# Weight blocks split into two parts in one step, and their products ordered by part

## The chip, the cores and the metric

The kernel runs on one core of a Trainium2 chip. The metric is the device time of one execution in microseconds; the time before is the median of three runs.

## The reference

One layer on 256 tokens of width 2048, all in float32: a normalisation, a projection `w_in` whose columns feed a gated delta net (8 heads of 128) and an RWKV7 part (16 heads of 64), an output projection `w_out`, a cross attention to 256 memory tokens (4 heads of 128), a feed-forward with squared ReLU, and a last normalisation:

```python
u = rmsnorm(h, mix_norm_w);  p = u @ w_in
o_dn = deltanet_group(p[..., :DN_COLS], ...)
o_rw = rwkv7_group(p[..., DN_COLS:], ...)
h = h + concatenate([o_dn, o_rw]) @ w_out
h = h + memory_cross_attention(rmsnorm(h), rmsnorm(mem), wq, wk, wv, wo)
h = h + square(relu(rmsnorm(h) @ ffn_w1)) @ ffn_w2       # 2048 -> 8192 -> 2048
return rmsnorm(h, final_norm_w)
```

## The kernel before

Every large product is made of float32r products. An operand x is split into a high part (x cast to float32r) and a low part (x less that, cast again); the sum of high x high, high x low and low x high stands for the float32 product. The activations are split once per use; the weights are split block by block as they come.

A block of weights is 512 KB, 128 partitions of 1024 values. `weights` loads it on SyncE's queue into one of five `raw` buffers (pool `wp`) and splits it in two steps of 512 values: a ScalarE copy (line 239) makes the high part `whi`, a VectorE subtraction (line 240, recorded at line 110 of the helper `tt`) the low part `wlo`. Each has three buffers (`WB`) of half a block. Loads and splits have a raised priority in the planner, the Tile framework's list scheduler, which sets the order on every engine from a simulated timeline.

`gemm` (line 244) computes 256 tokens by 512 columns into two PSUM banks, one for each 128 tokens. A block holds two k tiles of 512 columns. For each k tile and each half of the tokens it issues three products with the activations as the stationary operand and 512 weight columns moving: high x `whi` (line 254), high x `wlo` (255), low x `whi` (256): twelve a block. `gemm` serves `w_in` (112 blocks), `w_out` (32), `wk`, `wq`, `wv`, `wo` (8 each) and the second feed-forward layer `w2` (120; its last 8 blocks go through `gemm_rows`, which the change leaves alone).

`gemm_T` (line 261) computes the first feed-forward layer transposed, 128 hidden columns a bank. Here the weights are stationary and the activations move; a block holds eight k tiles of 128 columns. For each k tile it issues the low part against the high activations, 256 wide (line 272), and the high part against both parts of the activations, 512 wide (line 273); only at the first k tile of a bank does the low one come second (line 275). Two blocks make a bank, four banks a call, 16 calls: 128 blocks.

The feed-forward goes in four rounds of four `gemm_T` calls (32 blocks) and four `gemm` calls (32 blocks). Before it stand the scans of the two mixing groups, whose small products the planner places between those of `w_in`, `wk` and `w_out`. For `wk` and `wv` the memory's transpose is loaded in four tiles each (line 995) through the same `raw` buffers, as are two tiles of the scans' outputs (line 980); at the start three of the five buffers hold weights of the low-rank projection (line 352). ScalarE and VectorE also scale, shift and take results from PSUM.

Of the kernel before, what the change touches and what calls it, by code (L numbers as in the profile page):

```python
# [17 lines left out]
P = 128  # L18
# [9 lines left out]
WB = 3  # L28
# [12 lines left out]
def host_layout(inp):  # L41
    a = {k: np.asarray(v) for k, v in inp.items()}
    x, mem = a["x"][0], a["mem"][0]
    f = np.float32

    def tr(t):
        return np.ascontiguousarray(t.T.reshape(NKT, P, S).transpose(1, 0, 2))

    def blocks(w, n=NB):
        k, cols = w.shape  # L50
        return np.ascontiguousarray(
            w.reshape(k // (KB * P), KB, P, cols // n, n).transpose(3, 0, 2, 1, 4))

    def blocks_T(w):
        """[512 columns, 128 columns, half of the k tiles, p, k tile, column]"""
        return np.ascontiguousarray(w.reshape(2, 8, P, w.shape[1] // NB, 4, P).transpose(3, 4, 0, 2, 1, 5))

    w_in = a["w_in"][0]
    DN, RW = 0, 4112
    order = []  # L60
    for g in range(2):
        for j in (0, 1):
            u = 2 * g + j
            order += list(range(RW + 256 * u, RW + 256 * (u + 1)))
            order += list(range(RW + 1024 + 256 * u, RW + 1024 + 256 * (u + 1)))
            if j == 0:
                order += list(range(RW + 2048 + 512 * g, RW + 2048 + 512 * (g + 1)))
    for g in range(2):
        for j in range(3):
            order += list(range(1024 * j + 512 * g, 1024 * j + 512 * (g + 1)))  # L70
    order += list(range(3072, 4096))
    lora = list(range(RW + 3072, RW + 3328)) + list(range(4096, 4112))

    def col(v):
        return v.reshape(-1, P).T

    mu = a["rw_mu"][0]
    cols = np.concatenate([
        col(a["mix_norm_w"][0]), col(a["xa_norm_w"][0]), col(a["mem_norm_w"][0]), col(a["ffn_norm_w"][0]),
        a["dn_conv_w"][0].reshape(4, 24, P).transpose(2, 1, 0).reshape(P, 96),  # L80
        col(mu[0:1024]), col(mu[1024:2048]), col(mu[2048:3072]), col(mu[3072:3328]),
        col(a["rw_w0"][0]), col(a["rw_a0"][0]), col(a["rw_k_k"][0]), col(a["rw_k_a"][0]),
        col(a["rw_ln_w"][0]), col(a["rw_ln_b"][0]), col(a["rw_r_k"][0].reshape(-1)), col(a["dn_norm_w"][0]),
    ], axis=1)
    i = np.arange(P)
    bones = (i[:, None] // 64 == i[None, :] // 64).astype(f)
    consts = np.concatenate([
        np.eye(P, dtype=f), (i[:, None] <= i[None, :]).astype(f), bones, np.ones((P, P), f),
        np.tile(np.eye(16, dtype=f).reshape(1, 256), (P, 1)),
        (i[:, None] // 64 == np.arange(2)[None, :]).astype(f),  # L90
        (i[:, None] // 16 % 2 == np.arange(2)[None, :]).astype(f)], axis=1)
    r = {
        "xT": tr(x), "memT": tr(mem), "x": x, "mem": mem,
        "w_lora": blocks(w_in[:, lora], LORA), "w_in": blocks(w_in[:, order]),
        "w_out": blocks(a["w_out"][0]), "wq": blocks(a["xa_wq"][0]), "wk": blocks(a["xa_wk"][0]),
        "wv": blocks(a["xa_wv"][0]), "wo": blocks(a["xa_wo"][0]),
        "w1": blocks_T(a["ffn_w1"][0]), "w2": blocks(a["ffn_w2"][0]),
        "cols": cols, "wa2": np.concatenate([a["rw_w2"][0], a["rw_a2"][0]]),
        "g2": a["rw_g2"][0], "dnrow": np.concatenate([a["dn_a_log"][0], a["dn_dt_bias"][0]])[None, :],
        "fnw": a["final_norm_w"][None, :], "consts": consts,  # L100
    }
    return {k: np.ascontiguousarray(v) for k, v in r.items()}


def body(ctx, tc, I, out, dbg=None, upto=99):
# [24 lines left out]
    wp = ctx.enter_context(tc.tile_pool(name="wp", bufs=5))  # L130
# [14 lines left out]
    def bank(tag=None):  # L145
        """a PSUM bank: three serve the large products, two each of two scans, one the projections."""
# [24 lines left out]
    # derived per-channel scalars  # L171
# [15 lines left out]
    def lhs_split(raws, wname, pool, tag):  # L187
        """raw^T (times the norm's weight) split in two float32r parts, four k tiles a tile, as they are asked for."""
# [16 lines left out]
    def gemm_rows(lhs, wblk, evac, kbs, his, los):  # L205
        """the same, the first 128 tokens before the others, from weights that all stay."""
# [21 lines left out]
    def weights(src, a, b, parts):  # L228
        """a block of weights [128, a, b] in two float32r parts."""
        with tc.high_priority(3000):  # L230
            raw = wp.tile([P, a, b], F32, tag="raw", name=nm("raw"))
            nc.sync.dma_start(out=raw, in_=src)
            res = []
            n = a // parts
            for q in range(parts):
                hi = wp.tile([P, n, b], F32R, tag="whi", bufs=WB, name=nm("whi"))
                lo = wp.tile([P, n, b], F32R, tag="wlo", bufs=WB, name=nm("wlo"))
                w = raw[:, q * n:(q + 1) * n]
                A.copy(hi, w)  # L239
                tt(lo, w, hi.bitcast(F32), ALU.subtract)  # L240
                res += [(hi[:, i], lo[:, i]) for i in range(n)]
        return res

    def gemm(lhs, wblk, n, evac, kbs=None):
        """[256 tok, n] = lhs^T @ W: three float32r products stand for the float32 one."""
        acc = [bank("g") for _ in range(2)]
        kbs = list(kbs if kbs is not None else range(NKT // KB))
        for kb in kbs:
            w = weights(wblk[kb], KB, n, KB)
            for q in range(KB):  # L250
                for m in range(2):
                    first, last = kb == kbs[0] and q == 0, kb == kbs[-1] and q == KB - 1
                    xh, xl = lhs(kb * KB + q, m)
                    T.matmul(acc[m][:, :n], lhsT=xh, rhs=w[q][0], start=first, stop=False)  # L254
                    T.matmul(acc[m][:, :n], lhsT=xh, rhs=w[q][1], start=False, stop=False)  # L255
                    T.matmul(acc[m][:, :n], lhsT=xl, rhs=w[q][0], start=False, stop=last)  # L256
                    if last:
                        evac(m, acc[m][:, :n])


    def gemm_T(rhs, wblk, evac):
        """(x W)^T in four parts of 128 columns, [128 col, (W x_hi, W_hi x_lo)]; rhs(kt) is (x_hi, x_lo)^T, 512 wide."""
        for j in range(4):
            acc = bank("g")
            for b in range(2):
                w = weights(wblk[j, b], 8, P, 2)
                for k in range(8):
                    first, last = b == 0 and k == 0, b == 1 and k == 7
                    x = rhs(8 * b + k)
                    xf = x.rearrange("p a t -> p (a t)")  # L270
                    if not first:
                        T.matmul(acc[:, 0:S], lhsT=w[k][1], rhs=x[:, 0], start=False, stop=False)  # L272
                    T.matmul(acc, lhsT=w[k][0], rhs=xf, start=first, stop=last)  # L273
                    if first:
                        T.matmul(acc[:, 0:S], lhsT=w[k][1], rhs=x[:, 0], start=False, stop=False)
# [23 lines left out]
    def rms(src, name):  # L299
        """1 / rms of the rows of src[:, m, :]."""  # L300
# [8 lines left out]
    def tpose4(o, ins):  # L309
        """up to four 128x128 transposes into one bank."""  # L310
# [50 lines left out]
    # the clock of the array rises and the functions' table loads while the first operands are on their way  # L361
# [73 lines left out]
    # gates of the deltanet: [tok, chunk, head]  # L435
# [35 lines left out]
    inv = [0]  # L471

    def inverse(B, pool, pool2):
        """B is overwritten with the inverse of I + (its strictly upper part); what lies below its diagonal is zero.

        X12 = -X11 B12 X22 for blocks of 2 to 128, the larger ones on tiles of the array."""
# [11 lines left out]
        def quarters(t, n):  # L488
            """the quarters 11, 12, 22 of the diagonal blocks of 2n: [q, block, row, column]."""
# [94 lines left out]
    def rw_shift(pt, c0, names, blks):  # L584
        """columns c0.. of the projection [tok, col] to shifted [col, tok] tiles of two blocks."""
# [12 lines left out]
    def rw_unit(u, r, k, v):  # L598
# [59 lines left out]
        # bonus * v  # L658
# [8 lines left out]
        # scores  # L667
# [21 lines left out]
        # [tok, .] forms  # L689
# [57 lines left out]
        # group norm, bonus, gate  # L747
# [94 lines left out]
    def dn_unit(g, kq, v2):  # L842
# [6 lines left out]
        # norms per token: [tok, (k/q), chunk, head]  # L849
# [21 lines left out]
        # decays, scores  # L871
# [72 lines left out]
        # norm over the head, times silu(z)  # L944
# [90 lines left out]
    def tok_T(src, wname):  # L1035
        """transposes of src [tok, 2048] (times the norm's weight), split in two parts, four k tiles a step."""
# [131 lines left out]
    def last(m, p):  # L1168
        """the last 512 columns in two halves, so that little is left to do once the second's sum of squares is there."""
# [55 lines left out]
```

## Time and profile before

| | |
|---|---|
| median of three runs | 1446.87 us (1446.61 to 1447.17) |
| profiled execution, from first to last instruction (span) | 1442.5 us |
| what the median has over this span | 4.4 us |
| TensorE, VectorE, ScalarE busy | 98%, 66%, 54% |
| TensorE weight loads busy | 81% |
| weight blocks that `weights` splits | 424 |
| instructions | 22496 |

The profile has no time of its own for the profiled execution beside its span, so the span is set against the median of the runs. A matmul's record lasts until its result is drained, so records overlap, and the pace of TensorE is read from start to start and not from their length.

### The profile page before, as it was taken

To read this page: it belongs to the slowest core of one execution; us is meant where nothing else is said; L and a number is where in the kernel's file an instruction comes from. 1 tells how busy PE (TensorE), PEld (TensorE's weight loads), DVE (VectorE), ACT (ScalarE), POOL (GpSimd) and SP (SyncE) were. 2 spreads that over 40 slices of the span, in tenths; PEclk is the share of its full clock that TensorE was granted. 3 is DMA by queue.
4 is the path that set the end of the run, shared out by engine and by line. 5 is a ranking of instruction groups with operands and counts; after the bars stand their busy time and mean duration, and the time that the engine had idled before them with its cause. 6 is when DMAs were issued, how large, how long until landed. Compare 5 with 4: busy or idle time off the path is not lost.

```text
span 1442.5 us, 22496 instructions
## 1 busy us (share of the span) xinstructions
PE 1414.8 (98%) x8284; PEld 1168.9 (81%) x8284; DVE 950.1 (66%) x1799; ACT 780.8 (54%) x1491; POOL 50.6 (4%) x66
## 2 busy tenths in 40 slices
PE   9999999999999989999999999999999999999997
PEld 7877788787876868887788888888888888888886
DVE  7748574869587685767676655666556665566664
ACT  7656454555456454566565544555445554455553
POOL 0010001100010000000000000000000000000000
PEclk9999999999999999999999999999999999999999
DMA  7444433454366464556465556555665555655554
GB/s 281 157 145 152 135 121 112 147 177 144 102 200 207 138 190 146 166 173 212 136 209 186 190 192 197 185 187 189 193 197 186 185 190 194 195 182 187 191 188 146
DMA packets 90688, 252.88 MB, mean 175 GB/s; under 512 B 20673, under 2 KB 29393, under 8 KB 90193
## 3 DMA queue, kind: packets, MB, share of 16 engines
q1 hardware_dynamic: 70304, 243.96, 51.2%
q10 hardware_dynamic: 19920, 6.42, 1.8%
q8 instruction: 65, 1.06, 0.3%
q0 software_dynamic: 352, 1.06, 0.2%
q14 instruction: 47, 0.38, 0.1%
HBM read 244.72 MB, written 6.69 MB: 174 GB/s over the span
## 4 chain that ended last, share of the span: by engine, by line
PE 82%; DMA 7%; DVE 6%; ACT 3%; issue 2%; SPq 0%; POOL 0%; ACTq 0%; POOLq 0%; DVEq 0%
PE ps_g L273 16%; PE ps_g L255 16%; PE ps_g L254 15%; PE ps_g L256 15%; PE ps_g L272 8%; DVE wlo L110 2%; PE ps_s L675 2%; DMA scr<-Sc 1%; DMA xc<-inv 1%; DMA mraw<-in_memT_dram 1%; PE ps_x L312 1%; DMA g<-scr 1%; DVE xtmp L110 1%; DMA junk<-in_mem_dram 1%; PE ps_s L312 1%
## 5 line engine op out<-in xcount | busy, mean ns | idle before, releaser
L110 DVE TENSOR_TENSOR wlo<-raw,whi 128x512 fp32r<-128x512 f32 x848 | 583.3, 691 | 388.1 <-ACT whi L239 386.8
L239 ACT CAST whi<-raw 128x512 fp32r<-128x512 f32 x848 | 523.4, 621 | 489.8 <-DVE wlo L110 203.7
L273 PE MATMUL ps_g<-hhl,whi 128*128 128x512 f32 x1024 | 357.6, 398 | 0.2 <-ACT whi L239 0.2
L272 PE MATMUL ps_g<-hhl,wlo 128*128 128x256 f32 x960 | 269.9, 281 | 0.0
L273 PEld LDWEIGHTS ps_g<-hhl,whi 128*128 128x128 f32 x1024 | 188.4, 188 | 42.5 <-ACT whi L239 0.5
L255 PE MATMUL ps_g<-wlo,xhl 128*128 128x512 f32 x512 | 209.9, 410 | 8.4 <-DVE wlo L110 8.3
L256 PE MATMUL ps_g<-whi,xhl 128*128 128x512 f32 x512 | 202.0, 395 | 0.0
L256 PE MATMUL ps_g<-whi,flo 128*128 128x512 f32 x480 | 186.7, 389 | 0.0
L255 PE MATMUL ps_g<-wlo,fhi 128*128 128x512 f32 x480 | 186.7, 389 | 0.0
L254 PE MATMUL ps_g<-whi,xhl 128*128 128x512 f32 x512 | 180.8, 406 | 3.4 <-ACT whi L239 3.4
L272 PEld LDWEIGHTS ps_g<-hhl,wlo 128*128 128x128 f32 x960 | 181.5, 189 | 2.8 <-ACT hhl L122 0.2
L254 PE MATMUL ps_g<-whi,fhi 128*128 128x512 f32 x480 | 151.3, 389 | 0.0
L255 PEld LDWEIGHTS ps_g<-wlo,xhl 128*128 128x128 f32 x512 | 96.6, 189 | 37.7 <-DVE wlo L110 18.2
L254 PEld LDWEIGHTS ps_g<-whi,xhl 128*128 128x128 f32 x512 | 94.6, 189 | 26.7 <-ACT whi L239 5.9
L256 PEld LDWEIGHTS ps_g<-whi,xhl 128*128 128x128 f32 x512 | 96.7, 189 | 18.8 <-issue 0.7
L255 PEld LDWEIGHTS ps_g<-wlo,fhi 128*128 128x128 f32 x480 | 90.1, 188 | 18.8
L256 PEld LDWEIGHTS ps_g<-whi,flo 128*128 128x128 f32 x480 | 90.1, 188 | 18.7
L254 PEld LDWEIGHTS ps_g<-whi,fhi 128*128 128x128 f32 x480 | 90.1, 188 | 18.6
L113 DVE SCALAR_TENSOR_TENSOR cy<-ps_x,colt,cy 128x255 f32<-128x255 f32 (+2 forms) x72 | 34.2, 476 | 10.9 <-ACT cy L122 10.3
L1191 ACT CAST fhi<-hid 128x256 fp32r<-128x256 f32 x64 | 26.1, 408 | 9.5 <-DVE hid L113 0.8
L113 DVE SCALAR_TENSOR_TENSOR hid<-hid 128x256 f32<-128x256 f32 x64 | 27.2, 425 | 2.2
L113 DVE SCALAR_TENSOR_TENSOR h<-ps_g,rf,h 128x512 f32<-128x512 f32 (+1 forms) x34 | 22.8, 712 | 8.0 <-PE ps_g L225 8.0
(360 smaller groups left out, 1540.7 us busy)
## 6 DMA issues: line engine op xcount, KB each, us to landing
raw<-in_w_dram SPq DMA_DIRECT2D x256, 512.0 KB, 3.5
raw<-in_w_in_dram SPq DMA_DIRECT2D x112, 512.0 KB, 3.5
raw<-in_w_out_dram SPq DMA_DIRECT2D x32, 512.0 KB, 3.5
raw<-in_wk_dram SPq DMA_DIRECT2D x8, 512.0 KB, 3.5
mraw<-in_memT_dram SPq DMA_DIRECT2D x8, 512.0 KB, 3.6
raw<-in_wq_dram SPq DMA_DIRECT2D x8, 512.0 KB, 3.4
raw<-in_wv_dram SPq DMA_DIRECT2D x8, 512.0 KB, 3.7
raw<-in_wo_dram SPq DMA_DIRECT2D x8, 512.0 KB, 3.5
```

Source lines behind the costliest of these rows:

```text
L110: return (e or V).tensor_tensor(o, a, b, op=op)
L113: return V.scalar_tensor_tensor(o, a, s, b, op0=op0, op1=op1)
L239: A.copy(hi, w)
L254: T.matmul(acc[m][:, :n], lhsT=xh, rhs=w[q][0], start=first, stop=False)
L255: T.matmul(acc[m][:, :n], lhsT=xh, rhs=w[q][1], start=False, stop=False)
L256: T.matmul(acc[m][:, :n], lhsT=xl, rhs=w[q][0], start=False, stop=last)
L272: T.matmul(acc[:, 0:S], lhsT=w[k][1], rhs=x[:, 0], start=False, stop=False)
L273: T.matmul(acc, lhsT=w[k][0], rhs=xf, start=first, stop=last)
L312: T.transpose(out=o[:, j * P:(j + 1) * P], in_=a, identity=ident)
L675: T.matmul(bb[hl][:, 256 * i:256 * i + 256], lhsT=BK[hs, j, i, cs], rhs=AR[hs, j, :, cs], start=True, stop=True)
L1191: A.copy(hi[:, j], t)
```

## The change

`weights` casts and subtracts a whole block in one instruction each, 1024 wide. Its two parts have two buffers of a whole block each instead of three of half a block, and the raw blocks four buffers instead of five. In both `gemm` and `gemm_T` the products with the high part of the whole block are issued first and those with the low part after them. In `gemm` a block is then four pairs of high x `whi`, low x `whi`, going through k tiles and token halves, and behind them the four high x `wlo`, the first token half's two before the second's. In `gemm_T` it is eight high products, 512 wide, and then eight low ones, 256 wide. Number and shapes of the products are the same.

```diff
-WB = 3
+WB = 2
-    wp = ctx.enter_context(tc.tile_pool(name="wp", bufs=5))
+    wp = ctx.enter_context(tc.tile_pool(name="wp", bufs=4))
-    def weights(src, a, b, parts):
+    def weights(src, a, b):
         with tc.high_priority(3000):
             raw = wp.tile([P, a, b], F32, tag="raw", name=nm("raw"))
             nc.sync.dma_start(out=raw, in_=src)
-            res = []
-            n = a // parts
-            for q in range(parts):
-                hi = wp.tile([P, n, b], F32R, tag="whi", bufs=WB, name=nm("whi"))
-                lo = wp.tile([P, n, b], F32R, tag="wlo", bufs=WB, name=nm("wlo"))
-                w = raw[:, q * n:(q + 1) * n]
-                A.copy(hi, w)
-                tt(lo, w, hi.bitcast(F32), ALU.subtract)
-                res += [(hi[:, i], lo[:, i]) for i in range(n)]
-        return res
+            hi = wp.tile([P, a, b], F32R, tag="whi", bufs=WB, name=nm("whi"))
+            lo = wp.tile([P, a, b], F32R, tag="wlo", bufs=WB, name=nm("wlo"))
+            A.copy(hi, raw)
+            tt(lo, raw, hi.bitcast(F32), ALU.subtract)
+        return hi, lo
 # gemm
-            w = weights(wblk[kb], KB, n, KB)
+            hi, lo = weights(wblk[kb], KB, n)
             for q in range(KB):
                 for m in range(2):
-                    first, last = kb == kbs[0] and q == 0, kb == kbs[-1] and q == KB - 1
                     xh, xl = lhs(kb * KB + q, m)
-                    T.matmul(acc[m][:, :n], lhsT=xh, rhs=w[q][0], start=first, stop=False)
-                    T.matmul(acc[m][:, :n], lhsT=xh, rhs=w[q][1], start=False, stop=False)
-                    T.matmul(acc[m][:, :n], lhsT=xl, rhs=w[q][0], start=False, stop=last)
+                    T.matmul(acc[m], lhsT=xh, rhs=hi[:, q], start=kb == kbs[0] and q == 0, stop=False)
+                    T.matmul(acc[m], lhsT=xl, rhs=hi[:, q], start=False, stop=False)
+            for m in range(2):
+                for q in range(KB):
+                    last = kb == kbs[-1] and q == KB - 1
+                    T.matmul(acc[m], lhsT=lhs(kb * KB + q, m)[0], rhs=lo[:, q], start=False, stop=last)
                     if last:
-                        evac(m, acc[m][:, :n])
+                        evac(m, acc[m])
 # gemm_T
-                w = weights(wblk[j, b], 8, P, 2)
+                hi, lo = weights(wblk[j, b], 8, P)
                 for k in range(8):
-                    first, last = b == 0 and k == 0, b == 1 and k == 7
-                    x = rhs(8 * b + k)
-                    xf = x.rearrange("p a t -> p (a t)")
-                    if not first:
-                        T.matmul(acc[:, 0:S], lhsT=w[k][1], rhs=x[:, 0], start=False, stop=False)
-                    T.matmul(acc, lhsT=w[k][0], rhs=xf, start=first, stop=last)
-                    if first:
-                        T.matmul(acc[:, 0:S], lhsT=w[k][1], rhs=x[:, 0], start=False, stop=False)
+                    T.matmul(acc, lhsT=hi[:, k], rhs=rhs(8 * b + k).rearrange("p a t -> p (a t)"),
+                             start=b == 0 and k == 0, stop=False)
+                for k in range(8):
+                    T.matmul(acc[:, 0:S], lhsT=lo[:, k], rhs=rhs(8 * b + k)[:, 0], start=False,
+                             stop=b == 1 and k == 7)
             evac(j, acc)
```

## Rows read from the trace of the kernel before

**Rows 1.** The page: busy time, share, instructions by engine; the chain's shares.

```profile
PE 1414.8 (98%) x8284; PEld 1168.9 (81%) x8284; DVE 950.1 (66%) x1799; ACT 780.8 (54%) x1491; POOL 50.6 (4%) x66
...
PE 82%; DMA 7%; DVE 6%; ACT 3%; issue 2%; SPq 0%; POOL 0%; ACTq 0%; POOLq 0%; DVEq 0%
```

**Rows 2.** Windows: stretch, length, busy PE, PEld, DVE, ACT, POOL; clock, DMA share, GB/s.

```profile
26.00:560.00 534.00, 522.05 (x3800) 416.69 (x3800) 371.02 (x797) 293.27 (x590) 44.93 (x52) 0.99 0.48 153
...
902.00:993.00 91.00, 91.00 (x517) 79.01 (x516) 60.91 (x112) 50.43 (x96) 0.00 (x0) 1.00 0.57 186
```

**Rows 3.** Waits, TensorE, 721 to 1425 us: us in total, times, longest.

```profile
PE ps_g L273 <- ACT whi L239: 0.2, 1, 0.2
```

**Rows 4.** Waits, whole span: those of TensorE for weight parts.

```profile
PEld ps_g L255 <- DVE wlo L110: 19.0, 29, 2.9
...
PE ps_g L255 <- DVE wlo L110: 8.3, 12, 2.5
...
PE ps_g L254 <- ACT whi L239: 3.4, 4, 1.6
```

**Rows 5.** Timeline, TensorE, first feed-forward layer: start, length, engine, line, tiles, shapes, count.

```profile
904.73 0.28 PE L272 MATMUL ps_g<-hhl,wlo 128*128 128x256 f32 x1
...
907.21 0.28 PE L272 MATMUL ps_g<-hhl,wlo 128*128 128x256 f32 x1
907.33 0.62 PE L273 MATMUL ps_g<-hhl,whi 128*128 128x512 f32 x2
907.79 0.28 PE L275 MATMUL ps_g<-hhl,wlo 128*128 128x256 f32 x1
907.91 0.28 PE L272 MATMUL ps_g<-hhl,wlo 128*128 128x256 f32 x1
908.03 0.40 PE L273 MATMUL ps_g<-hhl,whi 128*128 128x512 f32 x1
908.26 0.28 PE L272 MATMUL ps_g<-hhl,wlo 128*128 128x256 f32 x1
```

**Rows 6.** Timeline, TensorE, end of a second-layer stage: first and last of ten products.

```profile
899.65 0.39 PE L255 MATMUL ps_g<-wlo,fhi 128*128 128x512 f32 x1
...
901.70 0.39 PE L256 MATMUL ps_g<-whi,flo 128*128 128x512 f32 x1
```

**Rows 7.** Timeline, TensorE, low-rank projection, 272 columns: first and last of nine.

```profile
12.58 0.29 PE L404 MATMUL ps_s<-whi,xhl 128*128 128x272 f32 x1
...
13.59 0.29 PE L404 MATMUL ps_s<-whi,xhl 128*128 128x272 f32 x1
```

**Rows 8.** Timeline, TensorE: a run of products one column wide, merged.

```profile
366.55 1.90 PE L857 MATMUL ps_s<-cons,sq 128*128 128x1 f32 x16
```

**Rows 9.** The page, costliest groups: count, busy us, mean ns, idle before.

```profile
L110 DVE TENSOR_TENSOR wlo<-raw,whi 128x512 fp32r<-128x512 f32 x848 | 583.3, 691 | 388.1 <-ACT whi L239 386.8
L239 ACT CAST whi<-raw 128x512 fp32r<-128x512 f32 x848 | 523.4, 621 | 489.8 <-DVE wlo L110 203.7
```

**Rows 10.** Timeline, ScalarE and VectorE: cast and subtraction 1024 wide.

```profile
519.71 1.05 ACT L982 CAST ohl<-oraw 128x1024 fp32r<-128x1024 f32 x1 [0.92 <-DMA oraw<-o_dram]
...
520.79 1.23 DVE L110 TENSOR_TENSOR ohl<-oraw,ohl 128x1024 fp32r<-128x1024 f32 x1 [1.28 <-ACT ohl L982]
```

**Rows 11.** Waits, whole span: ScalarE for weight buffers and for the memory's tiles.

```profile
ACT whi L239 <- PE ps_g L256: 164.5, 198, 2.6
ACT whi L239 <- PE ps_g L273: 106.2, 194, 1.1
...
ACT xhl L122 <- DMA mraw<-in_memT_dram: 9.9, 5, 4.3
```

**Rows 12.** Timeline, around a tile of the memory's transpose in `wv`.

```profile
657.19 0.33 SPq L995 DMA_DIRECT2D mraw<-in_memT_dram  x1
...
661.93 1.71 ACT L122 ACTIVATE xhl<-mraw,colt 128x256 fp32r<-128x256 f32 x4 [2.09 <-DMA mraw<-in_memT_dram]
...
664.20 0.77 PE L254 MATMUL ps_g<-whi,xhl 128*128 128x512 f32 x2 [1.62 <-ACT whi L239]
```

More of the change, by code (lines that the diff above doesn't have):

```diff
@@ L232, in weights @@
             nc.sync.dma_start(out=raw, in_=src)
-            res = []
-            n = a // parts
-            for q in range(parts):
-                hi = wp.tile([P, n, b], F32R, tag="whi", bufs=WB, name=nm("whi"))
-                lo = wp.tile([P, n, b], F32R, tag="wlo", bufs=WB, name=nm("wlo"))
-                w = raw[:, q * n:(q + 1) * n]
-                A.copy(hi, w)
-                tt(lo, w, hi.bitcast(F32), ALU.subtract)
-                res += [(hi[:, i], lo[:, i]) for i in range(n)]
-        return res
+            hi = wp.tile([P, a, b], F32R, tag="whi", bufs=WB, name=nm("whi"))
[3 more added lines that the diff above has]
+        return hi, lo
     def gemm(lhs, wblk, n, evac, kbs=None):
-        acc = [bank("g") for _ in range(2)]
+        acc = [bank("g")[:, :n] for _ in range(2)]
         kbs = list(kbs if kbs is not None else range(NKT // KB))
         for kb in kbs:
-            w = weights(wblk[kb], KB, n, KB)
+            hi, lo = weights(wblk[kb], KB, n)
             for q in range(KB):
                 for m in range(2):
-                    first, last = kb == kbs[0] and q == 0, kb == kbs[-1] and q == KB - 1
                     xh, xl = lhs(kb * KB + q, m)
-                    T.matmul(acc[m][:, :n], lhsT=xh, rhs=w[q][0], start=first, stop=False)
-                    T.matmul(acc[m][:, :n], lhsT=xh, rhs=w[q][1], start=False, stop=False)
-                    T.matmul(acc[m][:, :n], lhsT=xl, rhs=w[q][0], start=False, stop=last)
+                    T.matmul(acc[m], lhsT=xh, rhs=hi[:, q], start=kb == kbs[0] and q == 0, stop=False)
[4 more added lines that the diff above has]
+                    T.matmul(acc[m], lhsT=lhs(kb * KB + q, m)[0], rhs=lo[:, q], start=False, stop=last)
                     if last:
-                        evac(m, acc[m][:, :n])
+                        evac(m, acc[m])
     def gemm_T(rhs, wblk, evac):
```

## The prediction

> **What bounds the kernel now.** I read the page from its top: TensorE is busy 98% of the span, VectorE 66%, ScalarE 54%, and the chain of work that ended last is TensorE for 82% [rows 1]. Then the busy time by stretches [rows 2]: from 26 to 560 us (projection products that fill the gaps between the scans) TensorE is busy 522 of 534 us, and in a stretch of the feed-forward (902 to 993 us, all first-layer products) 91.0 of 91.0. From 721 to 1425 us, the whole feed-forward, TensorE waits for a weight part once, for 0.2 us [rows 3]. So in the feed-forward nothing but the time from one product to the next counts; before it a few stalls are left. Those that end with the weight parts are 8.3 us in 12 waits for the low part and 3.4 us in 4 for the high part at the products, and 19.0 us for the low part at the weight loads, which partly lie under a product that is still running [rows 4]. A busy TensorE is not one at its peak, so I went on to the timeline of starts.
>
> **Part 1, the order in the first feed-forward layer (lines 261 to 276).** Same 2048 products, other order. Now a 256-wide low and a 512-wide high product alternate: seven pairs from 904.73 to 907.21 us, 2.48 / 7 = 0.354 us a pair, so 8 x 0.354 = 2.83 us a block [rows 5]. After the change a block has eight high products in a row, then eight low ones; one change from low to high stays. What each costs in a row of its own kind:
> - High after high: 512-wide products of the second layer run at (901.70 - 899.65) / 9 = 0.228 us [rows 6], and the two high products in a row at a bank's start take 0.46 us together, 907.33 to 907.79 [rows 5]. I take 0.228. The alternating order thus pays 0.354 - 0.228 = 0.126 us for each low product.
> - Low after low: the trace has two in a row at each bank's start (64 times; one stands at 907.79). From the first low product to the next low one behind the high it takes 0.47 us [rows 5]; less the pair of 0.354 us, the second low product adds 0.116 us. Longer runs of short products are there only at the start, 272 columns wide: 12.58 to 13.59 us for eight, 0.126 us each [rows 7], or 0.119 us if it goes by columns (x 256 / 272). A run that is nothing but weight loads, 16 products one column wide, takes 1.90 us with its last drain [rows 8], at most 0.119 us each, so the loads don't forbid such a pace. From below I take 0.112 us, the reading error of the 0.47 us allowed for; from above 0.126 us, what the alternating order pays. I choose 0.116, the row of the very same shape, which is also within the scaled run.
>
> A block is then 7 x 0.228 + 0.354 + 7 x 0.116 = 2.762 us: 0.072 us less, x 128 blocks = 9.2 us. With 0.112 us it is 12.5 us (0.354 x 8 - 2.734 = 0.098 a block), with 0.126 us nothing.
>
> The Trainium skill's page "TensorE: Matmul & The Clock Gate", section "Back-to-back issue gap", gives a warm gap of N / 2.4 + 2.5 ns that knows no order of widths. By it a pair takes 216 + 109 = 325 ns in whatever order, and this part would be worth nothing. The trace disagrees on the size, with 0.354 us a pair [rows 5], and whether the order is free no run of before shows for more than two low products.
>
> **Part 2, the order in the other products (lines 244 to 259).** All are 512 wide before and after, twelve a block, with a weight load each: nothing at 0.228 us each. What moves is when the low part is first wanted: not behind one high product any more but behind eight, 7 x 0.228 = 1.6 us later. Against that the whole block is cast at once: 1.05 us instead of 0.62 for ScalarE, and 1.23 instead of 0.69 for VectorE [rows 9, 10], so the first high part comes 0.43 us later and the first low part 0.43 + 0.54 = 0.97 us later. A low-part stall thus shrinks by about 0.6 us. The 12 waits [rows 4] are 8.3 us as shown, with some 0.16 us each of a product's drain on top, about 10 us; with 12 x 0.6 off, but short ones ending at zero, I reckon 6.5 us saved. The high-part waits grow by 0.43 us: the 4 there are, 1.7 us, and perhaps half of the 12 places where the low part was late, 2.4 us. Net -2.4 us; bounds -10 (all low-part stalls go, no high one grows) and +5 (none goes, 12 places pay 0.43).
>
> **Part 3, half the instructions.** 848 casts and 848 subtractions [rows 9] become 424 each: ScalarE saves 2 x 0.621 - 1.05 = 0.19 us a block, 81 us in all, VectorE 2 x 0.691 - 1.23 = 0.15 us, 64 us [rows 9, 10]. I price it at nothing: under the feed-forward TensorE hides it (one wait of 0.2 us [rows 3]), before 560 us it lies beside the 522 us of products [rows 2]. A scan's instruction may now stand behind a 1.05 or 1.23 us one; its wait is covered by the same products.
>
> **Part 4, buffers.** The pairs go from three half blocks to two whole ones, in the same memory. Before the change ScalarE waits for TensorE to give a part back, 106.2 and 164.5 us in all [rows 11], so it is the buffers, not ScalarE, that set when a cast runs. After the change a high buffer is free behind its eight high products (1.8 us into a block) and is wanted two blocks (5.5 us) after the block's start: 3.7 us for a 1.05 us cast. Before the change it is two halves, 2.7 us, for a 0.62 us cast. Nothing is lost here.
>
> The raw blocks go from five buffers to four; tiles of the memory's transpose (line 995) and of the scans' outputs use the same ring on SyncE's queue. Where such a tile stands in the ring, its load is issued one block later, and behind it in ScalarE's order the casts wait. The trace has one such place: the load was issued at 657.19, ScalarE was idle 2.09 us for it until 661.93, and TensorE lost 1.62 us before 664.20 [rows 12]. A block lasts 12 x 0.228 = 2.7 us. Six such loads are in question (three each in the two products with the memory), so the cost is between 0 and 6 x 2.7 = 16 us. I take 2.7: ScalarE waits for five of these loads today, 9.9 us in all [rows 11], and of that 1.62 us, a sixth, reached TensorE; a sixth of 16 us is 2.7.
>
> **The sum.** 1442.5 of span - 9.2 - 2.4 + 2.7 = 1433.6 us. The median of the runs, 1446.87, is 4.4 us above this span (what lies around it, which the change doesn't touch): 1438.0 us, the forecast.
>
> **Rivals.**
> - *Nothing in the order.* Low products in a row cost the 0.126 us they cost now, since it is the load of 128 x 128 weights, one for each, that paces them. For it: the 272-wide run's 0.126 us [rows 7] would be the load's. Against it: the second of two low products added 0.116, and one-column products came at 0.119 or less [rows 5, 8]. Part 1 is nothing, the rest -2.4 + 2.7: 1447.2 us. The Trainium skill's gap rule above would give the same.
> - *Everything goes well.* Low products at 0.112 us (-12.5) and the low-part stalls mostly gone (-5), the ring free: 1429.4 us.
> - *Slower: the ring of four.* In the two products with the memory each of the six tiles arrives a block later and TensorE stops for it: +16.4 us, part 1 -9.2, part 2 -2.4: 1451.7 us. It decides from where a load's issue plus 4.7 us (657.19 to 661.93 [rows 12]) plus four scaling steps (1.7 us) is later than the end of the blocks in hand. For it: that place is late today. Against: elsewhere several blocks wait in the ring.
> - *The order isn't what the text says.* The planner could place low products back between high ones. The products of one bank accumulate in their written order, so for the first layer (one bank) that is excluded; with two banks only the order between the banks is free. 1447, as with the first rival.
>
> **How the numbers follow.** Forecast 0.50, everything well 0.13, nothing in the order 0.20 (with the last rival), ring 0.13; 0.04 is for scan work that the planner places otherwise, to either side. Measurements of this kernel can tell about 0.2% (2.9 us) from no change. Faster than 1444.0: forecast, everything well and half of the 0.04, 0.65; within 0.2%: 0.20; slower than 1449.8: the ring and the other half, 0.15. The range leaves out 2 in 10: from 1429 (nearly all of "everything well") to 1449 (all but the ring).
>
> **What would show it.** A first-layer block of 2.76 us, so a stage of 32 blocks 2.3 us shorter; low products starting 0.116 us apart, high ones 0.228. Casts of 1.05 and subtractions of 1.23 us, 424 each. Waits of the products for the low part mostly gone, those for the high part somewhat longer. The second layer's stages unchanged. Wrong it would be if the low products start 0.126 us or more apart, or if the waits behind the memory's tiles grow by several us.

## The result and the profile after

The changed kernel takes 1457.26 us (median), the one before 1447.02 us in the same runs: ratio 1.0075, 95% interval 1.0051 to 1.0099. It is slower by about 0.75%, where 1438 us was forecast. The profiled execution has a span of 1454.2 us.

The page of the changed kernel, busy time and costliest groups (they answer to [rows 1] and [rows 9]):

```profile
PE 1414.9 (97%) x8284; PEld 1179.2 (81%) x8284; DVE 902.1 (62%) x1375; ACT 700.3 (48%) x1067; POOL 56.3 (4%) x66
...
L110 DVE TENSOR_TENSOR wlo<-raw,whi 128x1024 fp32r<-128x1024 f32 x424 | 519.2, 1225 | 383.9 <-ACT whi L235 354.0
L235 ACT CAST whi<-raw 128x1024 fp32r<-128x1024 f32 x424 | 445.0, 1050 | 520.3 <-PE ps_g L250 293.2
```

The change does what it says: 424 casts of 1.05 us and 424 subtractions of 1.23 us, ScalarE 80 us and VectorE 48 us less busy (its subtractions alone 64 us). TensorE is as busy as before, and the span is 11.7 us longer.

Where that lies, by windows of TensorE. The columns are stretch, length, busy time, granted clock, DMA share and GB/s. The first stretch is from 26 us to the point where the first feed-forward layer goes on behind the last transposes of its input, at 726.5 us before and 742.4 us after (its very first products start some 4 us earlier, at 722.0 and 738.5 us); then come one stage of 32 blocks of the first layer and one of the second. First before, then after:

```profile
26.00:726.50 700.50, 684.53 (x4583) 1.00 0.49 157
1079.30:1169.70 90.40, 90.40 (x514) 1.00 0.57 188
1169.70:1256.70 87.00, 87.00 (x386) 1.00 0.59 193
```

```profile
26.00:742.40 716.40, 688.18 (x4580) 0.98 0.48 154
1092.90:1182.30 89.40, 89.40 (x514) 1.00 0.58 189
1182.30:1269.30 87.00, 87.00 (x386) 1.00 0.60 193
```

A stage of the first layer is 1.0 us shorter, one of the second as long as it was: over the four rounds some 4 us are gained. All that stands before the feed-forward takes 15.9 us longer (716.4 - 700.5), and that is the result: TensorE is idle there 28.2 us (716.4 - 688.2) instead of 16.0, and 3.7 us longer busy.

The waits of TensorE in that stretch after the change (us in all, times, longest) show what it waits for; before, 11.7 of its 15.4 us of waits were for the weight parts [rows 4]:

```profile
PE ps_s L306 <- DVE ob L110: 8.6, 1, 8.6
PE ps_g L254 <- DVE wlo L110: 6.7, 7, 2.2
PE ps_s L726 <- DVE ze L110: 6.1, 1, 6.1
PE ps_g L249 <- ACT whi L235: 2.3, 3, 1.0
```

The weight parts now cost 9.0 us (6.7 + 2.3). New are two long waits for the scans: 6.1 us for `ze` of an RWKV unit and 8.6 us for `ob`, the output of the last delta-net unit. Windows of the changed kernel show what stands at each, and at one shorter stretch (PE, PEld, DVE, ACT, POOL busy, then the clock):

```profile
325.00:342.10 17.10, 13.96 (x57) 13.11 (x58) 10.97 (x31) 3.86 (x7) 0.00 (x0) 0.50 0.04 4
...
601.50:611.70 10.20, 3.47 (x11) 2.49 (x12) 5.84 (x11) 1.96 (x3) 1.64 (x1) 0.50 0.16 50
...
680.00:683.40 3.40, 3.40 (x11) 2.72 (x10) 1.29 (x4) 1.04 (x1) 0.00 (x0) 0.50 0.75 217
```

The granted clock is at 0.50, 1.2 GHz, for 30.7 us in these three. Before the change there were two such stretches of 3.4 us up to the feed-forward:

```profile
372.90:376.30 3.40, 3.40 (x13) 2.87 (x12) 2.80 (x9) 1.15 (x2) 3.21 (x2) 0.50 0.00 0
465.10:468.50 3.40, 3.40 (x10) 2.76 (x11) 1.43 (x5) 1.76 (x4) 0.00 (x0) 0.50 0.77 272
```

Products take nearly twice as long at half clock (rows in the last section), so as an estimate half of the busy time there is lost: (13.96 + 3.47 + 3.40) / 2 = 10.4 us against 3.4, 7 us more. With the 12.2 us more of idle time that is 3 us more than the 15.9; where the 3 us were gained was not followed up.

The first long wait, in the timeline of the changed kernel:

```profile
315.20 0.37 ACTq L474 DMA_DIRECT2D scr<-Sc  x1
...
316.65 0.75 SPq L1049 DMA_DIRECT2D h<-in_x_dram  x1
...
318.77 0.63 ACTq L476 DMA_DIRECT2D g<-scr  x1
...
326.25 0.17 DVE L117 TENSOR_SCALAR x<-g 64x8 f32<-64x8 f32 x1 [7.65 <-DMA g<-scr]
...
326.90 0.41 DVE L110 TENSOR_TENSOR ze<-ps_s,nsg 128x256 f32<-128x256 f32 x1
```

The next unit's inverse begins with a 512 KB store to a scratch buffer in HBM, issued by ScalarE at 315.20 us, and a 64 KB load from it, issued at 318.77. Between the two, at 316.65, SyncE issues the 2 MB load of the residual, which takes 9.4 us to land (below, from the list of transfers: KB, and us from issue to landing). The small load lands behind the large one, after 7.5 us. VectorE stands still for it in its own order, and `ze`, which TensorE waits for, is three instructions behind. In the kernel before the residual's load was issued ahead of the store and held that up, also by 8 us (11.7 instead of 3.7), but VectorE did not wait for the load behind it. The residual's load in the changed kernel, then the timeline before:

```profile
h<-in_x_dram SPq DMA_DIRECT2D x1, 2048.0 KB, 9.4
```

```profile
300.10 0.43 SPq L1055 DMA_DIRECT2D h<-in_x_dram  x1
302.01 0.37 ACTq L480 DMA_DIRECT2D scr<-Sc  x1
...
313.74 0.65 ACTq L482 DMA_DIRECT2D g<-scr  x1
...
316.97 0.16 DVE L117 TENSOR_SCALAR x<-g 64x8 f32<-64x8 f32 x1
```

The second long wait, in the timeline of the changed kernel:

```profile
598.48 1.06 PE L927 MATMUL ps_s<-vv,At 128*128 128x128 f32 x8
...
604.13 1.64 POOL L110 TENSOR_TENSOR rr<-ms,pw 128x8 f32<-128x8 f32 x1 [39.46 <-DVE ms L118]
...
607.26 1.29 DVE L110 TENSOR_TENSOR ob<-ob,zs 128x512 f32<-128x512 f32 x2
608.09 2.05 PE L306 MATMUL ps_s<-cons,ob 128*128 128x128 f32 x8 [8.56 <-DVE ob L110]
```

Behind the last scan's last products (from 598.5 us) stand the norm over the head and the gate, 8.6 us over VectorE, ScalarE and GpSimd, and TensorE has nothing left for that time: the next products of the output projection need their result. Some later ones don't (those of three more column groups with the first delta-net unit, and `wv`), but they are written behind these; whether they could stand here was not tried. Before the change the same chain was there, but large products were left over to cover it. To see how many, I counted the large products up to the last scan step, in windows of the tile `ps_g` (the number behind x). First before, then after:

```profile
0.00:581.90 581.90, 408.34 (x1602) 0.99 0.49 159
```

```profile
0.00:598.40 598.40, 414.55 (x1656) 0.99 0.49 158
```

1656 are written ahead of the first one that needs the last scan's output. Of these, 54 were left before the change and none after it.

### The profile page after: what moved, and what is told of

It reads as the page before. It is cut to its first block, busy times and chain, and to the rows that moved or that the text cites. A ratio compares the mean times of both kernels' runs of the same rounds, so it can differ in the third digit from the quotient of the medians.

```text
span 1454.2 us, 21209 instructions
## 1 busy us (share of the span) xinstructions
PE 1414.9 (97%) x8284; PEld 1179.2 (81%) x8284; DVE 902.1 (62%) x1375; ACT 700.3 (48%) x1067; POOL 56.3 (4%) x66
## 5 line engine op out<-in xcount | busy, mean ns | idle before, releaser
L110 DVE TENSOR_TENSOR wlo<-raw,whi 128x1024 fp32r<-128x1024 f32 x424 | 519.2, 1225 | 383.9 <-ACT whi L235 354.0
L235 ACT CAST whi<-raw 128x1024 fp32r<-128x1024 f32 x424 | 445.0, 1050 | 520.3 <-PE ps_g L250 293.2
L265 PE MATMUL ps_g<-hhl,whi 128*128 128x512 f32 x1024 | 257.0, 392 | 0.2 <-DVE hhl L113 0.2
L249 PE MATMUL ps_g<-whi,xhl 128*128 128x512 f32 x512 | 207.1, 404 | 1.0 <-ACT whi L235 1.0
L250 PE MATMUL ps_g<-whi,xhl 128*128 128x512 f32 x512 | 203.2, 397 | 0.0
L249 PE MATMUL ps_g<-whi,fhi 128*128 128x512 f32 x480 | 186.8, 389 | 0.0
L254 PE MATMUL ps_g<-wlo,xhl 128*128 128x512 f32 x512 | 148.8, 404 | 6.6 <-DVE wlo L110 6.4
L268 PEld LDWEIGHTS ps_g<-hhl,wlo 128*128 128x128 f32 x1024 | 139.7, 190 | 10.0
L268 PE MATMUL ps_g<-hhl,wlo 128*128 128x256 f32 x1024 | 142.8, 282 | 0.0
L254 PE MATMUL ps_g<-wlo,fhi 128*128 128x512 f32 x480 | 130.1, 389 | 0.0
L669 PE MATMUL ps_s<-AR,BK 64*128 64x256 f32 x128 | 29.0, 403 | 0.0
```

The source lines that it names most:

```text
L110: return (e or V).tensor_tensor(o, a, b, op=op)
L235: A.copy(hi, raw)
L249: T.matmul(acc[m], lhsT=xh, rhs=hi[:, q], start=kb == kbs[0] and q == 0, stop=False)
L250: T.matmul(acc[m], lhsT=xl, rhs=hi[:, q], start=False, stop=False)
L254: T.matmul(acc[m], lhsT=lhs(kb * KB + q, m)[0], rhs=lo[:, q], start=False, stop=last)
L265: T.matmul(acc, lhsT=hi[:, k], rhs=rhs(8 * b + k).rearrange("p a t -> p (a t)"), start=b == 0 and k == 0, stop=False)
```

## The experiments

The theories: *width* (1024-wide instructions hold up the scans), *ring* (four raw buffers), *placement* (the planner puts the large products further ahead of the scans; by the products' order, or by the *depth* of the split buffers), and *collision* (the residual's load in front of the scan's). Each ratio is to the kernel before, run together with it. "First layer from" means the point behind the last transposes that ended the first stretch above (726.5 us before); some of the expectations name the very first product instead (722.0).

| run | ratio (95%) | large products before the last scan step | wait before the last transposes |
|---|---|---|---|
| changed kernel | 1.0075 (1.0051 to 1.0099) | 1656 | 8.6 us |
| half casts | 1.0005 (0.9983 to 1.0028) | 1656 | 8.4 us |
| old order, whole casts | 1.0014 (0.9990 to 1.0037) | 1585 | none |
| late residual | 1.0006 (0.9979 to 1.0034) | 1656 | 8.6 us |
| first layer only | 0.9983 (0.9958 to 1.0007) | 1602 | none |
| fill | 1.0049 (1.0028 to 1.0070) | 1656 | filled |
| ring of four | 0.9987 (0.9964 to 1.0010) | 1587 | none |
| first layer, late residual | 0.9977 (0.9958 to 0.9997) | 1572 | none |
| late residual and fill | 0.9994 (0.9969 to 1.0020) | 1656 | filled |
| four halves | 1.0011 (0.9990 to 1.0033) | 1656 | 8.5 us |
| new order, three halves | 1.0005 (0.9980 to 1.0029) | 1600 | none |
| two halves | 1.0491 (1.0452 to 1.0529) | 1464 | none |
| four halves, late residual | 0.9964 (0.9943 to 0.9986) | 1656 | 8.5 us |
| the same and first layer | 0.9959 (0.9940 to 0.9977) | 1656 | 8.5 us |

**Width: half casts.** The changed kernel with

```diff
+            n = a // 2
+            for q in range(2):
+                s = slice(q * n, (q + 1) * n)
+                A.copy(hi[:, s], raw[:, s])
+                tt(lo[:, s], raw[:, s], hi[:, s].bitcast(F32), ALU.subtract)
```

> The changed kernel, but each weight block is cast and subtracted in two halves of 512 into the same whole-block buffers; product order, two buffers and four raw buffers stay. If the 1024-wide instructions hold up the scans (theory: width), the first feed-forward layer begins near 722 us again instead of 738.5 and the time is near 1443. If the new order of the products and the buffers make the planner place the scans later (theory: placement), the first layer still begins between 734 and 742 us, TensorE still has waits of several us before it, and the time is 1453 to 1460. The first-layer stages stay at 89.3 us either way.

Measured 1.0005 (1448.92 us), first layer from 736.6 us: between the two. The 8.4 us wait and the 1656 products are still there; the wait near 321 us is not. Width alone is not the cause of the second wait.

**Order: the old one with whole casts.** In `gemm` high x high, high x low and low x high k tile by k tile again, the rest as changed.

> The changed kernel with whole-block casts, two buffers and four raw buffers, but the 512-wide products of gemm again go k tile by k tile as before (high x high, high x low, low x high); only the first layer keeps the new order. Placement by product order: the first layer begins near 724 us, time near 1444. Width, buffers or ring: it begins near 738, time near 1457. In between means that both have a part.

Measured 1.0014, first layer from 736.7 us, and neither long wait. What it has instead are six stretches at half clock of 3.4 us and waits of about 2 us. Either part of the change taken back gives most of the time back, which neither theory alone had expected.

**Collision: late residual.** The changed kernel with

```diff
+    A.copy(h[:, 0, 0:1], zs[:, 0, 0:1])
     nc.sync.dma_start(out=h, in_=x_tok)
```

> The changed kernel with the 2 MB load of the residual held back until the gate z is there (one copied column makes it wait), so that it no longer stands before the scan's own load at 318.8 us. Theory: the 6.2 us wait at 321 us and the 17 us at half clock behind it come from that load; without it both go, the first layer begins 12 to 15 us earlier, the time is near 1444. Rival: the scans are late by the order of TensorE's queue alone, TensorE then stops elsewhere, and the time stays above 1452.

Measured 1.0006, 1446.89 us: 10 us back. The wait for `ze` falls from 6.1 to 1.4 us, the 17.1 us at half clock is gone, the 8.6 us wait stays with its 10.2 us at half clock. The first layer goes on from 730.9 us. TensorE's order is the same as in the changed kernel up to 473 us, so the end of the wait near 321 us is the load's doing; behind that the order differs a little, so the time of this run is not the load's alone.

**Collision with the order unchanged: four halves, and four halves with the late residual.** The kernel before with

```diff
-WB = 3
+WB = 4
-    wp = ctx.enter_context(tc.tile_pool(name="wp", bufs=5))
+    wp = ctx.enter_context(tc.tile_pool(name="wp", bufs=4))
```

and the same with the added line above.

> The kernel before with four buffers of half a block for each split part instead of three, and four raw buffers; order of the products and width of the casts as before. Theory depth: deeper split buffers let the planner run the products ahead of the scans, so the last scan ends after the products that could cover it; the first layer begins near 736 us instead of 726, with a wait of several us before the last transposes and a stretch at half clock behind it, and the time is 1452 to 1456. Theory order: nothing changes, 1445 to 1449.

> Four half buffers and four raw ones, as in the run with four halves, and the residual's load held back; TensorE's order up to the feed-forward is the same as there, instruction for instruction, so that only the place of that load differs. Theory collision: the wait near 320 us (4.6 us) and the stretch at half clock behind it (13.7 us) go, the first layer begins near 727 instead of 738, and the time is 1441 to 1446. The wait of 8.5 us before the last transposes stays, as the order is the same. If the wait near 320 us stays too, the load was not its cause.

Four halves: 1.0011 (1451.69 us), not told from no change. All 1656 products stand ahead of the last scan step, the 8.5 us wait is there, and so is the collision. VectorE and TensorE around it, first with four halves, then with the late residual too:

```profile
322.77 0.17 DVE L117 TENSOR_SCALAR x<-g 64x8 f32<-64x8 f32 x1 [8.25 <-DMA g<-scr]
...
324.63 0.79 PE L255 MATMUL ps_g<-wlo,xhl 128*128 128x512 f32 x1 [4.59 <-DVE wlo L110]
```

```profile
317.28 0.17 DVE L117 TENSOR_SCALAR x<-g 64x8 f32<-64x8 f32 x1 [3.15 <-DMA g<-scr]
...
321.10 0.43 PE L732 MATMUL ps_s<-ze,Sc 128*128 128x64 f32 x2 [0.99 <-DVE ze L110]
```

With the same order on TensorE up to the feed-forward, instruction for instruction, VectorE's wait falls from 8.25 to 3.15 us and TensorE's of 4.59 us goes. The ratio falls from 1.0011 to 0.9964. So the load is the cause of the wait near 320 us; this is shown. The run also beats the kernel before and the changed one, although its 8.5 us wait stays. The first products of the first layer start only 3.5 us earlier in the two profiled executions (727.3 and 730.8 us), not 11 as expected. The 13.7 us at half clock behind the wait are gone, but the profiled execution with the late residual is the slowest of its twelve, and it has 13.7 us at half clock in another place (last section).

**Order with three halves.** The kernel before with all eight high products of a block ahead of its four low ones in `gemm`; three half buffers, five raw ones and half casts stay.

> The kernel before, with three half buffers, five raw buffers and half casts, but in the 512-wide products the new order: all eight high products of a block, then its four low ones. Theory depth: the scans stay nearly where they were, the first layer begins between 724 and 729 us, 1445 to 1449. Theory order: the products run ahead, the first layer begins near 736 and there is a long wait before the last transposes: 1453 to 1457.

Measured 1.0005, first layer from 730.5 us, 1600 products, no wait before the last transposes. The order alone does not run the products ahead.

**Two halves.** The kernel before with `WB = 2`.

> The kernel before with two buffers of half a block for each split part instead of three. Theory depth, other direction: the scans come earlier in TensorE's order (the last scan's gates after 942 products instead of 1112) and the last transposes are well covered, but the products wait for their parts more often, in the feed-forward too: the first layer begins between 725 and 760 us, and the time is above 1460. If depth did nothing, 1447.

Measured 1.0491. 1464 products stand ahead of the last scan step: depth moves the placement in both directions, 1464, 1602, 1656 for two, three, four halves (the last with four raw buffers, which alone give 1587). A first-layer stage takes 100.7 us instead of 90.4, so its time says nothing on the scans.

**Fill.** The changed kernel with 36 products of 128 columns behind the last scan's last product, results unread.

> The changed kernel with 36 more small products, whose result is not read, right behind the last scan's last product, so that TensorE works through the 8.7 us in which it waits at 599 us. They move nothing else in time: the chain over VectorE, ScalarE and GpSimd to the transposes stays 8.7 us long. If the wait costs its own length only, the time stays near 1457. If it also costs the 10.2 us at half clock behind it, that stretch goes and some 5 us with it: 1452.

Measured 1.0049, 1454.32 us: some 3 us less than the changed kernel, with intervals that overlap. The window in which the wait was now reads

```profile
599.00:611.00 12.00, 11.88 (x91) 10.56 (x90) 5.98 (x11) 3.87 (x7) 1.64 (x1) 1.00 0.15 45
```

The clock stays at 1.00, so the 10.2 us at half clock came from the idle time. It was worth some 3 us, not 5; with only 3.47 us busy in that stretch, not more than 2 us were to be had by the reckoning above. The wait for the chain stays as long as it was, it is only filled. With the late residual as well no gain can be told:

> The changed kernel with both cures: the residual's load held back and 36 small products behind the last scan's last product. The first cure alone gave 1446.9, the second alone 3 us. If the two losses are separate, 1443 to 1445; if the second was only a follow-up of the first, 1447.

Measured 0.9994, 1447.66 us against 1446.89 without the fill; the two cures don't add.

**Ring of four.** The kernel before with four raw buffers.

> The kernel before with four raw buffers instead of five and nothing else changed; its order on TensorE is the same as before up to some scan steps of the last scan. Theory ring (the prediction's slower rival): waits behind the tiles of the memory's transpose grow, the first layer begins up to 16 us later, time up to 1463. Theory placement: no change, 1445 to 1449.

Measured 0.9987: no cost. The prediction's slower rival falls.

**What paces low products.** The changed kernel with low products of the first layer 128 wide; it leaves out the low weight part for half of the tokens. One execution.

> The changed kernel with the low products of the first layer 128 columns wide instead of 256 (the low weight part of the second 128 tokens is left out). It tells what paces a run of low products: if it is the columns, they start 0.06 us apart and the eight take half of the 0.95 us; if it is the load of the weights, one for each, they stay near 0.11 to 0.12 us apart and the block stays near 2.79 us.

Timeline of the changed kernel, then of this one (start, length, products merged):

```profile
1101.26 2.00 PE L265 MATMUL ps_g<-hhl,whi 128*128 128x512 f32 x8
1103.10 1.12 PE L268 MATMUL ps_g<-hhl,wlo 128*128 128x256 f32 x8
1104.05 2.00 PE L265 MATMUL ps_g<-hhl,whi 128*128 128x512 f32 x8
```

```profile
1100.76 1.00 PE L268 MATMUL ps_g<-hhl,wlo 128*128 128x128 f32 x8
1101.61 2.07 PE L265 MATMUL ps_g<-hhl,whi 128*128 128x512 f32 x8
1103.51 1.00 PE L268 MATMUL ps_g<-hhl,wlo 128*128 128x128 f32 x8
```

Eight low products take 0.95 us with 256 columns, 0.119 each, and still 0.85 us with half the columns; the block goes from 2.79 (1101.26 to 1104.05) to 2.75 us. So at 128 columns it is not the columns that pace them. What each product has besides is one load of weights, so the loads are the likely pace, at about 0.11 us (argued, not shown by itself), and 256 columns lie just above that.

**The first layer alone, and with the late residual.** The kernel before with the new `gemm_T`, whole-block casts into buffers of its own (pool `fp`).

> The kernel before with only the first feed-forward layer changed: whole-block cast and subtraction into two buffers of their own, eight high products and then eight low ones. What stands before the feed-forward has the same order on TensorE as before. By the trace of the changed kernel a first-layer stage takes 89.3 us instead of 90.4: 4 x 1.1 = 4.4 us, so 1442.5. By the prediction's price it would be 9.2 us, 1437.8. If the order is worth nothing, 1447.

> The kernel before with the new order in the first layer alone and the load of the residual held back until the gate z is there. Of before's front the collision of that load with the scan's store (11.7 us instead of 4 at 302 us) goes, and its order on TensorE changes from there on. If the collision cost before as it cost after, some 3 to 8 us more are gained than with the first layer alone: 1438 to 1442. If TensorE had enough other products there, nothing: 1444 to 1446.

Measured 0.9983 (1446.05 us), not told from no change nor from the 4 us, and 0.9977 (1444.90 us), a gain of 0.03 to 0.42%. With three halves the late residual brings little: there the residual's load holds up the store, and TensorE had no long wait for it.

**All that helped.** Four halves, late residual, new order in the first layer.

> The run before this one (four half buffers, residual's load held back, old product order) with the first layer's new order from a pair of whole-block buffers of its own. If the first layer's gain of 4 x 1.1 us adds to it, 1439 to 1441 and clearly faster than before; if a deeper first layer moves the planner's order in front, anything up to 1447.

Measured 0.9959 (1442.93 us against 1448.26): the fastest here. The 8.5 us wait and the 1656 products are as before, and the first layer's part is no longer told from noise beside 0.9964.

## Why the prediction was wrong

- **What bounds the kernel.** Right for the feed-forward: its second layer didn't move, its first moved by the pace of the products. For the stretch before it I read "522 of 534 us busy" [rows 2] as cover that stays. It was the outcome of one order, and the change made another.
- **Part 1, first layer: -9.2 us.** Right in kind, mis-sized. A block went from 2.83 to 2.79 us instead of 2.76, some 4 us in all. The high products take 0.230 us each (1.84 / 8) rather than 0.228, the low ones 0.119 rather than 0.116. The run of 272 columns, scaled to 256 [rows 7], had 0.119; the couple [rows 5] was too short to show a run's pace. The rival *nothing in the order* had a pace that doesn't go by columns, and at half the columns there is one, at about 0.11 us; but 256 columns lie above it, and the order was worth 4 us.
- **Part 2, weight waits: -2.4 us.** The net came out, by luck: at the products the waits fell from 11.7 to 9.0 us, in 10 instead of 16. But those for the low part fell by 1.6 us (8.3 to 6.7) and not by 6.5, and those for the high part fell by 1.1 us (3.4 to 2.3) instead of growing by 4.1.
- **Part 3, half the instructions: nothing.** The step that failed. "A scan's instruction may now stand behind a 1.05 or 1.23 us one; its wait is covered by the same products" took the cover for given. Two waits for the scans, 6.1 and 8.6 us, and the half clock behind them (7 us by the estimate above) took the gain and more.
- **Part 4, buffers: "nothing is lost here".** Failed as well, in its first half: I asked whether a cast comes in time, not what the planner does with deeper buffers. With room for two blocks instead of one and a half it issues all 1656 large products before the last scan step, 54 more, and none is left for the last 8.6 us. The runs with two, three and four halves show that depth alone can do it, and the run with three halves that the new order alone does not. But two whole blocks in the old order have 1585, so with whole casts the new order is needed too; that a buffer's depth counts by how long the products hold it would explain this, and is argued, not shown.
- **Part 4, ring: +2.7 us.** Not there: 0.9987 (0.9964 to 1.0010) for the ring alone, where 2.7 us would be 1.0019. In the changed kernel ScalarE's waits for the memory's tiles did grow, from 9.9 to 13.0 us, but TensorE has no long wait behind them.
- **The rivals.** The slower one had the wrong mechanism. The one on the planner looked only at the order within a block; the planner's order between large products and scans is where the time went, and I gave it 0.04.

How the 0.75% divides: without the collision the changed kernel is at 1.0006, so the collision and the half clock behind it are most of it. At 1.0006 the first layer's gain of some 4 us is still lost again in front. The last wait is the longest one left there, but what it costs by itself was not shown: the fill covers it without shortening it, and four halves with the late residual beat the kernel before in spite of it.

Whether the collision strikes TensorE goes by the moment at which the residual's load is issued. In the four runs that have it between the scan's store and its load (changed kernel, fill, narrow low products, four halves) the small load takes 7.2 to 7.6 us, and VectorE waits 7.7 to 8.3 us for it. In the seven that have it ahead of the store (kernel before, half casts, old order, first layer only, ring of four, new order with three halves, two halves) the store holds up the small load's issue by 8 to 14 us, against 3.4 with the residual late, and VectorE waits at most 2.4 us. The old order as an example:

```profile
316.60 0.43 SPq L1047 DMA_DIRECT2D h<-in_x_dram  x1
318.61 0.37 ACTq L472 DMA_DIRECT2D scr<-Sc  x1
...
328.80 0.63 ACTq L474 DMA_DIRECT2D g<-scr  x1
...
334.24 0.16 DVE L117 TENSOR_SCALAR x<-g 64x8 f32<-64x8 f32 x1
```

This goes with what the runs of the two parts show: taking back either the wide casts or the order puts the load ahead of the store, and gives most of the time back. Why the planner places it so was not settled. Open is also why four halves, with the collision and the last wait as in the changed kernel, are at 1.0011 and not at 1.0075, and what keeps the changed kernel with the late residual (1.0006) above four halves with the late residual and the first layer (0.9959). The waits for weight parts beside the collision are longer with whole casts in the new order, 9.0 us against 4.3 with four halves, which is a part of it; width of the casts and order of the products differ between the two.

## What to carry to other kernels

Where a planner mixes a long dependent chain with large independent work, a change that lets the large work run freer need not shorten the stretch: here it used the cover up early, and the chain's end stood bare. Busy time read before the change is cover only for that order; count the large products ahead of the chain's last step, before and after. And look for a large load that nobody is in a hurry for in front of a small one that stands ahead of the chain in an engine's order: holding it back was worth some 0.7% in the changed kernel and 0.5% with four halves, and little with three, where it stood in front of a store.

## What the runs showed of the hardware

A long idle time cost more than itself: behind the 6.1 us wait TensorE ran at 0.50 of its clock until 342.1 us, 14.7 us longer than the wait. With the idle time filled, the half clock before the last transposes did not come.

The half clock also came without any idle time. In the run with four halves and the late residual TensorE was busy throughout, with products one column wide (16 from 378.1, 16 more from 385.1 us) among small ones, and the clock stood at 0.50 for 13.7 us. First this run, then the one with four halves, where the same products follow in the same order (the one-column ones from 388.4 and 392.5 us) and the clock stayed at 1.00; windows as above, and from the timeline one group of products in each:

```profile
366.00:379.00 13.00, 13.00 (x90) 10.78 (x88) 8.75 (x15) 7.62 (x14) 0.00 (x0) 1.00 0.50 162
379.00:392.70 13.70, 13.70 (x58) 12.75 (x57) 3.54 (x11) 2.21 (x4) 3.27 (x2) 0.50 0.01 2
...
383.04 1.81 PE L719 MATMUL ps_s<-r,Sc 128*128 128x64 f32 x8
```

```profile
382.50:397.00 14.50, 14.50 (x111) 13.12 (x110) 6.46 (x14) 6.36 (x12) 2.34 (x2) 1.00 0.23 76
...
391.39 1.00 PE L719 MATMUL ps_s<-r,Sc 128*128 128x64 f32 x8
```

The same eight products of 64 columns take 1.81 us at half clock and 1.00 at full. So the order of the products alone doesn't settle where the clock falls. How much half clock an execution has differs from one to the next, and its time with it: among the twelve with the late residual the slowest took 1449.08 us at a mean granted clock of 0.987, the fastest 1437.82 us at 0.994; the median is 1443.58 us. So one profiled execution can't be set against another by its half clock alone.

A transfer of one queue held up one of another: ScalarE's 64 KB load took 7.5 us behind SyncE's 2 MB load in the changed kernel, and 3.0 us with that load held back.
